# Row gathers for 32 more tokens in a product-key expert mixer: dense up products over 352 columns, 76 parked blocks, transposes in the norms

## The chip, the cores and the metric

The kernel runs on one core of a Trainium2 chip. The metric is device time in microseconds of one launch, taken as the median of several runs. The core has a matrix engine (TensorE, PE in the profile, PEld for its weight loads), a vector engine (VectorE, DVE), an activation engine (ScalarE, ACT), GpSimd (POOL) and a sync engine (SyncE, SP). Here SP issues all plain transfers, and POOL issues the gathers. The engines run their own lists of instructions in order and wait for one another by semaphores.

## What is computed

An encoder trunk of two layers over 512 tokens of width 1024. Layer 0 mixes tokens by neighbourhood attention, layer 1 by a short gated convolution. After each mixer comes the same kind of channel mixer, and nearly all of the time goes there:

```python
def peer_mixer(h, w_query, sub_keys, w_up, w_down):
    ...
        q = (xc @ w_query).reshape(c, PEER_HEADS, 2, PEER_HALF_DIM).astype(jnp.float32)
        sc = jnp.einsum('chpd,hpnd->chpn', q, keys32)
        sv, si = lax.top_k(sc, PEER_TOPK)
        cand = (sv[:, :, 0, :, None] + sv[:, :, 1, None, :]).reshape(c, PEER_HEADS, -1)
        cidx = (si[:, :, 0, :, None] * PEER_N_KEYS + si[:, :, 1, None, :]).reshape(c, PEER_HEADS, -1)
        best, pos = lax.top_k(cand, PEER_TOPK)
        eidx = jnp.take_along_axis(cidx, pos, axis=-1)
        g = jax.nn.softmax(best, axis=-1)
        u = w_up[eidx]
        a = jnp.einsum('cd,chkd->chk', xc, u).astype(jnp.float32)
        act = (jax.nn.gelu(a, approximate=False) * g).astype(xc.dtype)
        vv = w_down[eidx]
        return jnp.einsum('chk,chkd->cd', act, vv)
```

There are 8 heads with the best 16 of 256 candidates each, so every token picks 128 of 16384 experts. An expert is one row of `w_up` and one row of `w_down`, 1024 floats each. Around each mixer stands a root-mean-square norm and a residual.

## The kernel before

**Tokens.** The 512 tokens are four chunks of 128. In the expert mixer (`peer`) the last chunk (c3) gathers its rows: for each of its 128 picks one indirect transfer fetches a row of `w_up` per token, DVE multiplies it with the normed token and sums (`gather_up`, L474), and later a row of `w_down` is fetched and added with the value as weight (`gather_down`, L484). The other 384 tokens (`TD`) go densely: all 16384 experts are computed for them, in 128 blocks of 128 experts, and a gate matrix that is zero where an expert wasn't picked removes the rest.

**Exact products.** Each f32 operand is split by `split` (L100) into a high part that ACT rounds and a low part that DVE takes as the difference (L106). A product is then three products: high with high, low with high, high with low.

**Retrieval stage.** `norm_t` (L159) makes the normed, transposed activations: per chunk a reciprocal root, a diagonal `dg` with it (L168), and 32 products of the chunk with the diagonal that turn and scale at once (L174); ACT and DVE evict them as `xh` and `xl`. Then 16 query blocks follow, each with key products (`ps_k`) and the two-step top 16 on DVE (`top16`, L590). `select` (L599) then picks the experts of a chunk on DVE, in the order 3, 0, 1, 2. For the dense chunks the gates are spread over a matrix: for each four tokens (a quad) DVE makes one-hot tiles `ob` and `oa`, PE multiplies them (`ps_gb`, L457), ACT evicts to `stage`, and SP stores to `gd` in DRAM.

**Blocks ahead.** While DVE selects, PE would have little to do. So `NPRE` = 52 dense up blocks run in the meantime; their results after Gelu are stored to `ad` in DRAM (parked) and read back later as `at`. How many pieces go between two steps of the retrieval is set by estimated costs on DVE and PE and `PRE_RATE`:

```python
            for d, p in retrieval():
                dve += d
                pe += p
                while pe < dve * PRE_RATE and next(pre, 0) is None:
                    pe += 0.49
```

The framework's scheduler then settles the order on each engine.

**Main stage.** The list `blocks` mixes fresh blocks (up products still to be done, `AHEAD` = 4 early) and parked ones in groups of four. `dense_down` (L508) multiplies a block's values with the gates `gt`, splits the result and a block of `w_down`, and adds 18 products over 512 columns to six accumulators (L536). The 256 gathers of chunk 3 are spread over the blocks (L577), two shares for a fresh block and one for a parked one, through four row buffers. An up block is 24 products over 384 columns (L127) from a 512 KB load. The loads of `w_up` and `w_down` have three buffers each (`RAW`), the split results two.

## Time and profile before

| what | us |
|---|---|
| median of 3 runs | 3028.08 |
| lowest and highest run | 3024.51, 3029.07 |
| profiled execution, its own time | 3023.92 |
| span of the profiled execution | 3022.1 |
| PE, DVE, ACT, POOL busy in it | 2985.9, 2337.9, 1362.3, 658.6 |

The page slices the span into 40 equal parts. A digit is the busy share of an engine in tenths, PEclk the granted clock of TensorE, DMA the mean busy share of the 16 DMA engines. The two layers show as two repeats: first a mixer with little transfer, then retrieval with a full DVE and an idle POOL, then the long main stage with POOL's gathers and transfers near their limit. A busy PE is not PE at its peak, since its records overlap (their ends are modelled); how fast it goes is read from the distance of one start to the next.

### The profile page before, as it was taken

How to read it: one execution, taken by the hardware profiler on the slowest of the kernel's cores; microseconds unless marked ns; L12 is line 12 of the kernel's file. 1: busy time of each engine (PE TensorE's matmuls, PEld its weight loads, DVE VectorE, ACT ScalarE, POOL GpSimd, SP SyncE). 2: the span in 40 equal slices, each digit the busy share in tenths (PEclk: the TensorE clock that was granted, in tenths of full speed). 3: DMA queues.
4: the chain of work that ended last, by engine and by line, in shares of the span. 5: the costliest groups of instructions: out<-in, count | busy, mean ns of one | idle time of the engine just before them, and what ended most of it. 6: DMA issues, size and time to landing. Idle time of an engine off the chain costs nothing. (4 is left out here: it accounts for less than half of the span.)

```text
span 3022.1 us, 44124 instructions
## 1 busy us (share of the span) xinstructions
PE 2985.9 (99%) x15730; PEld 2677.1 (89%) x15730; DVE 2337.9 (77%) x5115; ACT 1362.3 (45%) x2237; POOL 658.6 (22%) x571
## 2 busy tenths in 40 slices
PE   8999999999999999999999999999999999999998
PEld 7887899999888888888888888999988888888887
DVE  4444899887888888887874489998788888888786
ACT  5444246996333333333342233599733333333333
POOL 0000000001434443443310000000034344444341
PEclk9999999999999999999999999999999999999999
DMA  4222244567999999998942323556699999999995
GB/s 162 95 97 89 87 138 159 220 233 282 340 344 340 337 344 338 333 338 316 340 144 92 108 93 114 171 196 232 239 358 340 334 348 335 340 326 350 324 332 192
DMA packets 297981, 747.96 MB, mean 247 GB/s; under 512 B 23456, under 2 KB 139168, under 8 KB 294688
## 3 DMA queue, kind: packets, MB, share of 16 engines
q1 hardware_dynamic: 224032, 476.67, 45.2%
q0 software_dynamic: 73728, 268.47, 24.0%
q8 instruction: 124, 2.03, 0.3%
q14 instruction: 97, 0.79, 0.1%
HBM read 672.17 MB, written 72.88 MB: 247 GB/s over the span
## 5 line engine op out<-in xcount | busy, mean ns | idle before, releaser
L127 PE MATMUL ps_up<-xhf,wu_l 128*128 128x384 f32 (+1 forms) x2304 | 798.9, 347 | 1.2 <-DVE wu_l L106 1.0
L127 PE MATMUL ps_up<-xhf,wu_h 128*128 128x384 f32 (+1 forms) x2304 | 794.2, 345 | 2.0 <-ACT ab L499 2.0
L127 PE MATMUL ps_up<-xlf,wu_h 128*128 128x384 f32 (+1 forms) x2304 | 792.0, 344 | 0.0
L105 ACT ACTIVATE wu_h<-wu_raw 128x1024 fp32r<-128x1024 f32 x336 | 355.4, 1058 | 710.6 <-PE ps_up L127 430.7
L470 POOL DMA_INDIRECT row<-in_up,eidx x256 | 322.4, 1260 | 1312.9 <-DMA wu_raw<-in_up_t 881.6
L536 PE MATMUL acc<-wd_h,w_l 128*128 128x512 f32 x1536 | 603.7, 393 | 0.1
L536 PE MATMUL acc<-wd_l,w_h 128*128 128x512 f32 x1536 | 599.0, 390 | 0.0
L105 ACT ACTIVATE wd_h<-wd_raw 128x1024 fp32r<-128x1024 f32 x256 | 271.6, 1061 | 702.0 <-issue 619.3
L106 DVE TENSOR_TENSOR wu_l<-wu_raw,wu_h 128x1024 fp32r<-128x1024 f32 x336 | 410.0, 1220 | 176.4 <-ACT wu_h L105 176.1
L536 PE MATMUL acc<-wd_h,w_h 128*128 128x512 f32 x1536 | 514.9, 392 | 0.0
L106 DVE TENSOR_TENSOR wd_l<-wd_raw,wd_h 128x1024 fp32r<-128x1024 f32 x256 | 313.3, 1224 | 235.5 <-ACT wd_h L105 234.9
L127 PEld LDWEIGHTS ps_up<-xhf,wu_h 128*128 128x128 f32 x2304 | 433.3, 188 | 21.1 <-ACT ab L499 3.3
L127 PEld LDWEIGHTS ps_up<-xlf,wu_h 128*128 128x128 f32 x2304 | 433.1, 188 | 17.5
L127 PEld LDWEIGHTS ps_up<-xhf,wu_l 128*128 128x128 f32 x2304 | 433.1, 188 | 17.2 <-DVE wu_l L106 3.7
L470 POOL DMA_INDIRECT row<-in_down,eidx x256 | 330.4, 1291 | 511.7 <-DVE sq L477 464.6
L536 PEld LDWEIGHTS acc<-wd_l,w_h 128*128 128x128 f32 x1536 | 288.4, 188 | 61.7
L486 DVE SCALAR_TENSOR_TENSOR accg<-row,ag,accg 128x1024 f32<-128x1024 f32 x256 | 327.4, 1279 | 16.1 <-DMA row<-in_down,eidx 15.5
L536 PEld LDWEIGHTS acc<-wd_h,w_l 128*128 128x128 f32 x1536 | 288.6, 188 | 55.0 <-DVE w_l L106 0.9
L536 PEld LDWEIGHTS acc<-wd_h,w_h 128*128 128x128 f32 x1536 | 287.2, 188 | 54.8
L477 DVE SCALAR_TENSOR_TENSOR sq<-row,hn 128x1024 bf16<-128x1024 f32 x256 | 312.0, 1219 | 3.9 <-DMA row<-in_up,eidx 2.7
L457 PE MATMUL ps_gb<-ob,oa 128*128 128x128 f32 x1536 | 209.6, 274 | 0.0
L458 ACT ACTIVATE stage<-ps_gb 128x512 f32<-128x512 f32 x192 | 204.6, 1114 | 2.1 <-PE ps_gb L457 1.5
(164 smaller groups left out, 3325.8 us busy)
## 6 DMA issues: line engine op xcount, KB each, us to landing
wd_raw<-in_down SPq DMA_DIRECT2D x256, 512.0 KB, 5.8
wu_raw<-in_up_t SPq DMA_DIRECT2D x256, 512.0 KB, 4.9
gd<-stage SPq DMA_DIRECT2D x24, 2048.0 KB, 7.4
gt<-gd SPq DMA_DIRECT2D x64, 768.0 KB, 9.2
ad<-ab SPq DMA_DIRECT2D x104, 192.0 KB, 2.1
at<-ad SPq DMA_DIRECT2D x52, 384.0 KB, 8.0
wu_raw<-in_w_query SPq DMA_DIRECT2D x32, 512.0 KB, 3.5
wu_raw<-in_w_qkv SPq DMA_DIRECT2D x24, 512.0 KB, 3.5
```

The costliest lines, as they stand in the source:

```text
L105: nc.scalar.activation(hi, raw, AF.Copy)
L106: nc.vector.tensor_tensor(lo, raw, hi.bitcast(F32), op=ALU.subtract)
L127: nc.tensor.matmul(ps[:, :n], a[:, c], b[:, kc, :n], start=k == 0, stop=k == 3 * KC - 1)
L457: nc.tensor.matmul(ps[:, n * NK:(n + 1) * NK], a, b4[:, n], start=True, stop=True)
L458: nc.scalar.activation(stage[:, :, 4 * q:4 * q + 4].rearrange("p i t -> p t i"), ps.rearrange("p (t i) -> p t i", t=4), AF.Copy)
L470: nc.gpsimd.indirect_dma_start(out=t, out_offset=None, in_=table, in_offset=bass.IndirectOffsetOnAxis(ap=eidx[:, k:k + 1], axis=0))
L477: nc.vector.scalar_tensor_tensor(o, t, 1.0, hn, op0=ALU.mult, op1=ALU.mult, accum_out=ag[:, k:k + 1])
L486: nc.vector.scalar_tensor_tensor(accg, t, ag[:, k:k + 1], accg, op0=ALU.mult, op1=ALU.add)
L536: nc.tensor.matmul(acc[c, half], aa[:, cs], ww[:, hs], start=new and i == 0, stop=n == NK - 1 and ww is held[-1][-1])
```

## The change

The last 32 tokens of the third chunk (`UT`, so the dense up products keep `TU` = 352 columns) get their values from gathered rows of `w_up`. Their down side stays dense: the value, Gelu times gate, is written into the gates `gT`, and the columns of the dense values are set to one (`ring`, `parked`). For this chunk 2 is selected first; its 32 tokens stand in a tile `hu` four times, one copy per group of 32 partitions, so that one indirect transfer brings 4 picks of 32 tokens, and 32 transfers bring all 128. `unit_steps` issues them between the steps of the other chunks' selection and multiplies on DVE; `unit_values` places the results ahead of the last group of quads. `hu` and the rows take buffers of the `w_down` splits and loads. `NPRE` goes to 76 and `PRE_RATE` to 1.52. In `norm_t` DVE scales the whole chunk (`hs`), and PE transposes it with the identity; the reciprocal root of chunk 3 is used again for `hn`.

```diff
-NPRE = 52
-PRE_RATE = 1.4
+NPRE = 76
+UN = 1
+UT = 32
+TU = TD - UN * UT
+GB = 4
+PRE_RATE = 1.52
...
-        dg = {}
-        for c in order:
-            r = rstd_of(c)
-            dg[c] = small.tile([P, P], F32, name="dg", bufs=4)
-            nc.vector.tensor_scalar(dg[c], ident, r, None, op0=ALU.mult)
-        for k0 in range(0, KC, 4):
-            ps = [ps_acc(f"ps_t{k}") for k in range(4)]
+        rs = {}
+        with tc.tile_pool(name="scaled", bufs=1) as sp:
+            hs = {}
             for c in order:
+                r = rs[c] = rstd_of(c)
+                hs[c] = sp.tile([P, D], F32, name=f"hs{c}")
+                nc.vector.tensor_scalar(hs[c], h[:, c], r, None, op0=ALU.mult)
+            for k0 in range(0, KC, 4):
+                ps = [ps_acc(f"ps_t{k}") for k in range(4)]
+                for c in order:
+                    for k in range(4):
+                        kc = k0 + k
+                        nc.tensor.transpose(ps[k][:, c * P:(c + 1) * P], hs[c][:, kc * P:(kc + 1) * P], ident)
                 for k in range(4):
                     kc = k0 + k
-                    nc.tensor.matmul(ps[k][:, c * P:(c + 1) * P], h[:, c, kc * P:(kc + 1) * P], dg[c],
-                                     start=True, stop=True)
-            for k in range(4):
-                kc = k0 + k
-                nc.scalar.activation(xh[:, kc], ps[k], AF.Copy, scale=gain[:, kc:kc + 1])
-                nc.vector.scalar_tensor_tensor(xl[:, kc], ps[k], gain[:, kc:kc + 1], xh[:, kc].bitcast(F32),
-                                               op0=ALU.mult, op1=ALU.subtract)
-        return xh, xl
+                    nc.scalar.activation(xh[:, kc], ps[k], AF.Copy, scale=gain[:, kc:kc + 1])
+                    nc.vector.scalar_tensor_tensor(xl[:, kc], ps[k], gain[:, kc:kc + 1], xh[:, kc].bitcast(F32),
+                                                   op0=ALU.mult, op1=ALU.subtract)
+        return xh, xl, rs
...
-    ad = dram.tile([NPRE // 2, P, 2, TD], F32, name="ad")
+    ad = dram.tile([NPRE // 2, P, 2, TU], F32, name="ad")
...
-            r3 = rstd_of(c3)
-            nc.vector.scalar_tensor_tensor(hn, h[:, c3], r3, hn, op0=ALU.mult, op1=ALU.mult)
+            nc.vector.scalar_tensor_tensor(hn, h[:, c3], rs[c3], hn, op0=ALU.mult, op1=ALU.mult)
+            cu = ND - 1
+            hu = []
+            for u in range(UN):
+                q = slice(P - (UN - u) * UT, P - (UN - u - 1) * UT)
+                t = wpool.tile([P, D], F32, name="hu", tag="wd_h", bufs=2)
+                nc.sync.dma_start(t[q], g_ffn_row[l].to_broadcast([UT, D]))
+                nc.vector.scalar_tensor_tensor(t[q], h[q, cu], rs[cu][q], t[q], op0=ALU.mult, op1=ALU.mult)
+                for g in range(P // UT):
+                    if g * UT != q.start:
+                        nc.scalar.activation(t[g * UT:(g + 1) * UT], t[q], AF.Copy)
+                hu.append((q, t))
...
+            fu = pp.tile([P, UN, UT], F32, name="fu")
+            xu = pp.tile([P, UN, UT], I32, name="xu")
+            gu = pp.tile([P, UN, UT], F32, name="gu")
+            au = pp.tile([P, UN, UT], F32, name="au")
+            urows = []
+            def flat_ids(eid, ii, jj):
+                nc.vector.scalar_tensor_tensor(eid, ii, float(NK), jj, op0=ALU.mult, op1=ALU.add)
+                if l:
+                    nc.vector.tensor_scalar(eid, eid, float(l * NK * NK), None, op0=ALU.add)
+            def unit_lists(gg, ii, jj):
+                flat_ids(eid, ii, jj)
+                for u, (q, _) in enumerate(hu):
+                    for g in range(P // UT):
+                        ks = slice(g * UT, (g + 1) * UT)
+                        nc.scalar.activation(fu[ks, u], eid[q, ks], AF.Copy)
+                        nc.scalar.activation(gu[ks, u], gg[q, ks], AF.Copy)
+                nc.vector.tensor_copy(xu, fu)
+            def unit_steps():
+                at = [(u, k) for u in range(UN) for k in range(UT)]
+                for n in range(len(at) + 2):
+                    if n < len(at):
+                        u, k = at[n]
+                        t = wpool.tile([P, D], F32, name="urow", tag="wd_r", bufs=RAW)
+                        nc.gpsimd.indirect_dma_start(
+                            out=t, out_offset=None, in_=up,
+                            in_offset=bass.IndirectOffsetOnAxis(ap=xu[:, u, k:k + 1], axis=0))
+                        urows.append(t)
+                    if n >= 2:
+                        u, k = at[n - 2]
+                        o = acts.tile([P, D], BF16, name="sq", tag="sq")
+                        nc.vector.scalar_tensor_tensor(o, urows.pop(0), 1.0, hu[u][1], op0=ALU.mult, op1=ALU.mult,
+                                                       accum_out=au[:, u, k:k + 1])
+                    yield
+            def unit_values():
+                nc.scalar.activation(au, au, AF.Gelu)
+                nc.vector.tensor_tensor(au, au, gu, op=ALU.mult)
+                ps = ps_acc("ps_u")
+                for u in range(UN):
+                    nc.tensor.transpose(ps[:UT, u * P:(u + 1) * P], au[:, u], ident)
+                for u in range(UN):
+                    for g in range(P // UT):
+                        ks = slice(g * UT, (g + 1) * UT)
+                        nc.scalar.activation(gT[ks, TU + u * UT:TU + (u + 1) * UT],
+                                             ps[:UT, u * P + g * UT:u * P + (g + 1) * UT], AF.Copy)
...
-                for c in (3, 0, 1, 2):
+                units = iter(())
+                for c in (cu, c3, 0, 1):
                     it = select(sv[:, c], si[:, c], pr, cand)
                     while True:
                         try:
                             yield next(it), 0.0
+                            for _ in itertools.islice(units, 1):
+                                yield 1.3, 0.0
...
-                            nc.vector.tensor_copy(t[:, c * P:(c + 1) * P], ps[:, n * P:(n + 1) * P])
+                            m = min(P, TU - c * P) if n == 0 else P
+                            nc.vector.tensor_copy(t[:, c * P:c * P + m], ps[:, n * P:n * P + m])
+                        if c == cu:
+                            unit_lists(gg, ii, jj)
+                            units = unit_steps()
                 for t0 in range(0, TD, GT):
+                    if t0 == TU:
+                        for _ in units:
+                            yield 1.3, 0.0
+                        unit_values()
...
+            ring = [pp.tile([P, TD], F32, name=f"ab{n}") for n in range(AHEAD + 2)]
+            for t in ring:
+                nc.gpsimd.memset(t[:, TU:], 1.0)
...
-                for ps in up_pieces(up_t[l, b], xh, xl, TD):
+                for ps in up_pieces(up_t[l, b], xh, xl, TU):
                     yield
-                a = pp.tile([P, TD], F32, name="ab", tag="ab", bufs=AHEAD + 2)
-                nc.scalar.activation(a, ps[:, :TD], AF.Gelu)
+                a = ring[b % len(ring)]
+                nc.scalar.activation(a[:, :TU], ps[:, :TU], AF.Gelu)
                 if b < NPRE:
-                    nc.sync.dma_start(ad[b // 2, :, b % 2], a)
+                    nc.sync.dma_start(ad[b // 2, :, b % 2], a[:, :TU])
...
-                    at = p2.tile([P, 2, TD], F32, name="at")
-                    nc.sync.dma_start(at, ad[b // 2])
+                    at = parked[b // 2 % 2]
+                    nc.sync.dma_start(at[:, :, :TU], ad[b // 2])
...
+            parked = [p2.tile([P, 2, TD], F32, name=f"at{n}", bufs=1) for n in range(2)]
+            for t in parked:
+                nc.gpsimd.memset(t[:, :, TU:], 1.0)
```

Two places where the order on an engine changes follow.

DVE, first layer, before: the second chunk's pick (`msk`) overlaps the third chunk's top 16 (`best`, `tk`, `pos`); `wu_l` is the low part of a dense up block.

```order
L637 TENSOR_TENSOR msk_4151<-msk_4151,ranks_83 128x2048
L596 MAX best_4330<-tk_4390 128x8
L596 MAX best_4330<-tk_4402 128x8
L597 MAX_INDEX pos_4331<-best_4330,tk_4368 128x8
L106 TENSOR_TENSOR wu_l_4438<-wu_raw_4435,wu_h_4437 128x1024
L638 TENSOR_TENSOR msk_4151<-msk_4151,ds_4118 128x2048
L597 MAX_INDEX pos_4331<-best_4330,tk_4390 128x8
L597 MAX_INDEX pos_4331<-best_4330,tk_4402 128x8
```

Between two splits stand only steps of the selection. The same place with the change; `urow` is a gathered row, `au` the sums.

```order
L722 TENSOR_TENSOR msk_4405<-msk_4405,ranks_83 128x2048
L464 SCALAR_TENSOR_TENSOR sq_4220,au_3619<-urow_4144,hu_2576 128x1024
L112 TENSOR_TENSOR wu_l_4528<-wu_raw_4525,wu_h_4527 128x1024
L681 MAX best_4642<-tk_4758 128x8
L681 MAX best_4642<-tk_4795 128x8
L681 MAX best_4642<-tk_4823 128x8
L723 TENSOR_TENSOR msk_4405<-msk_4405,ds_4348 128x2048
L464 SCALAR_TENSOR_TENSOR sq_4248,au_3619<-urow_4181,hu_2576 128x1024
L682 MAX_INDEX pos_4643<-best_4642,tk_4758 128x8
L682 MAX_INDEX pos_4643<-best_4642,tk_4795 128x8
L682 MAX_INDEX pos_4643<-best_4642,tk_4823 128x8
L112 TENSOR_TENSOR wu_l_4565<-wu_raw_4562,wu_h_4564 128x1024
```

Row products now stand between the selection's steps and the splits, about one per split.

SP, main stage of the first layer, before: the loads of up blocks (`wu_raw`), down blocks (`wd_raw`), gates (`gt`) and parked pairs (`at`).

```order
L516 DMA at_9880<-ad_126 128x768
L111 DMA wu_raw_10018<-in_up_t 128x1024
L111 DMA wd_raw_9635<-in_down 128x1024
L111 DMA wd_raw_9706<-in_down 128x1024
L511 DMA gt_9878<-gd_125 128x12x128
L516 DMA at_9950<-ad_126 128x768
L111 DMA wd_raw_9777<-in_down 128x1024
L111 DMA wd_raw_9846<-in_down 128x1024
L111 DMA wd_raw_9888<-in_down 128x1024
L111 DMA wu_raw_10088<-in_up_t 128x1024
```

Here one group of parked blocks stands between groups of fresh ones. And with the change, where two groups of parked blocks follow each other:

```order
L598 DMA at0_8097<-ad_126 128x2x352
L117 DMA wu_raw_10495<-in_up_t 128x1024
L117 DMA wd_raw_9943<-in_down 128x1024
L117 DMA wd_raw_9978<-in_down 128x1024
L598 DMA at1_8098<-ad_126 128x2x352
L593 DMA gt_10106<-gd_125 128x12x128
L117 DMA wd_raw_10013<-in_down 128x1024
L117 DMA wd_raw_10045<-in_down 128x1024
L598 DMA at0_8097<-ad_126 128x2x352
L117 DMA wu_raw_10569<-in_up_t 128x1024
```

There are 38 loads of parked pairs per layer instead of 26 and fewer loads of up blocks among them. On PE, 80 up blocks stand ahead of the first down product in each layer's list, 59 before.

## Rows read from the trace of the kernel before

**Rows 1.** Stretches: us, busy PE, PEld, DVE, ACT, POOL (count), clock, DMA share, GB/s.

```profile
305.00:734.00 429.00, 427.47 (x2661) 410.74 (x2660) 382.34 (x1387) 282.91 (x456) 3.90 (x4) 1.00 0.50 176
734.00:1500.00 766.00, 766.00 (x3742) 680.25 (x3741) 626.89 (x819) 274.09 (x402) 312.52 (x245) 1.00 0.94 341
1500.00:1555.00 55.00, 54.95 (x242) 44.70 (x241) 42.52 (x61) 21.73 (x32) 9.59 (x7) 1.00 0.60 210
```

**Rows 2.** Waits of PE: who, for whom, us in total, times, longest.

```profile
PE ps_t L174 <- DVE dg L168: 19.6, 4, 8.4
...
PE ps_up L127 <- DVE wu_l L106: 1.0, 4, 0.3
```

**Rows 3.** The chain that ended last: start, us, what.

```profile
2376.05 4.12 PE acc L536 x18
2380.18 4.19 PE ps_up L127 x24
```

**Rows 4.** Stretches as in the first group, in the selection of the first layer.

```profile
475.00:500.00 25.00, 24.00 (x139) 23.42 (x138) 25.00 (x98) 16.50 (x23) 0.00 (x0) 1.00 0.51 169
500.00:525.00 25.00, 25.00 (x161) 24.90 (x160) 24.22 (x62) 18.81 (x23) 0.00 (x0) 1.00 0.45 149
```

**Rows 5.** Instructions of PE in order of time: start, us, what, count.

```profile
107.22 0.66 PE L280 MATMUL ps_pt<-ident,sc 128*128 128x128 f32 x4
107.63 0.48 PE L127 MATMUL ps_up<-xlm,wu_h 128*128 128x512 f32 x1
...
600.91 1.05 PE L457 MATMUL ps_gb<-ob,oa 128*128 128x128 f32 x8
601.72 0.42 PE L127 MATMUL ps_up<-xhf,wu_l 128*128 128x384 f32 x1
...
1559.18 4.29 PE L174 MATMUL ps_t<-dg,h 128*128 128x128 f32 x36 [1.43 <-DVE dg L168]
```

**Rows 6.** Groups of DVE by line and form: busy us, mean ns, idle before.

```profile
L106 DVE TENSOR_TENSOR wu_l<-wu_raw,wu_h 128x1024 fp32r<-128x1024 f32 x336 | 410.0, 1220 | 176.4 <-ACT wu_h L105 176.1
...
L477 DVE SCALAR_TENSOR_TENSOR sq<-row,hn 128x1024 bf16<-128x1024 f32 x256 | 312.0, 1219 | 3.9 <-DMA row<-in_up,eidx 2.7
...
L477 DVE DVE_READ_ACCUMULATOR sq<-row,hn 128x1 f32 x256 | 20.9, 82 | 0.0
...
L168 DVE TENSOR_SCALAR dg<-ident,r 128x128 f32<-128x128 f32 x16 | 4.4, 282 | 0.0
L360 DVE TENSOR_SCALAR cv<-u,wc 128x512 f32<-128x512 f32 x8 | 3.9, 486 | 0.8
```

**Rows 7.** A group of ACT by line and form, as above.

```profile
L150 ACT ACTIVATE sq<-h 128x1024 bf16<-128x1024 f32 x22 | 23.1, 1052 | 13.2 <-DVE h L588 8.7 <-DMA h<-in_x 2.2 <-DVE h L583 2.0
```

**Rows 8.** Stretches as in the first group, in the norm after the attention.

```profile
284.00:290.00 6.00, 1.11 (x6) 0.58 (x4) 5.03 (x18) 5.73 (x13) 1.39 (x2) 0.86 0.79 220
290.00:295.00 5.00, 5.00 (x23) 5.00 (x24) 3.47 (x18) 1.38 (x4) 0.00 (x0) 0.50 0.22 79
295.00:300.00 5.00, 5.00 (x41) 4.78 (x40) 2.73 (x5) 3.46 (x7) 0.00 (x0) 0.98 0.02 3
```

**Rows 9.** Instructions of DVE in order of time, as for PE.

```profile
286.84 1.22 DVE L106 TENSOR_TENSOR wd_l<-wd_raw,wd_h 128x1024 fp32r<-128x1024 f32 x1
287.97 0.21 DVE L151 TENSOR_SCALAR v<-v 128x1 f32<-128x1 f32 x2
```

**Rows 10.** Issues of transfers: what, queue, count, KB each, us to landing.

```profile
at<-ad SPq DMA_DIRECT2D x52, 384.0 KB, 8.0
...
row<-in_up,eidx POOLq DMA_INDIRECT x256, 7.1
```

**Rows 11.** Stretches as in the first group, early in the two main stages.

```profile
750.00:775.00 25.00, 25.00 (x121) 21.85 (x120) 19.72 (x27) 9.01 (x13) 9.49 (x8) 1.00 1.05 408
2200.00:2225.00 25.00, 25.00 (x122) 21.94 (x121) 21.06 (x30) 8.46 (x14) 10.24 (x8) 1.00 1.01 392
```

More of the change, by code (lines that the diff above doesn't have):

```diff
@@ L204, in attention @@
     def attention(l):
-        xh, xl = norm_t(gm[:, l], f"m{l}", (3, 0, 1, 2) if l else range(NCH))
+        xh, xl, _ = norm_t(gm[:, l], f"m{l}", (3, 0, 1, 2) if l else range(NCH))
         with tc.tile_pool(name="attn", bufs=1) as ap, tc.tile_pool(name="attn2", bufs=2) as a2:
@@ L343, in short_conv @@
     def short_conv(l):
-        xh, xl = norm_t(gm[:, l], f"m{l}", (3, 0, 1, 2) if l else range(NCH))
+        xh, xl, _ = norm_t(gm[:, l], f"m{l}", (3, 0, 1, 2) if l else range(NCH))
         with tc.tile_pool(name="conv", bufs=1) as ap, tc.tile_pool(name="conv2", bufs=2) as a2:
@@ L373, in encoder @@
     gd = dram.tile([TD // GT, P, NK, GT], F32, name="gd")
-    ad = dram.tile([NPRE // 2, P, 2, TD], F32, name="ad")
+    ad = dram.tile([NPRE // 2, P, 2, TU], F32, name="ad")
     def peer(l):
-        xh, xl = norm_t(gf[:, l], f"f{l}")
+        xh, xl, rs = norm_t(gf[:, l], f"f{l}")
         with ExitStack() as st:
@@ L425, in retrieval @@
                     if c == c3:
-                        nc.vector.scalar_tensor_tensor(eid, ii, float(NK), jj, op0=ALU.mult, op1=ALU.add)
-                        if l:
-                            nc.vector.tensor_scalar(eid, eid, float(l * NK * NK), None, op0=ALU.add)
+                        flat_ids(eid, ii, jj)
                         nc.vector.tensor_copy(eidx, eid)
@@ L460, in retrieval @@
                         yield 1.35, 0.9
+                        for _ in itertools.islice(units, 1):
+                            yield 1.3, 0.0
                     nc.sync.dma_start(gd[t0 // GT], stage)
```

## The prediction, made before the changed kernel ran

> **What bounds the kernel now.** I read the busy times by stage first [rows 1]. The three stretches are the first layer's expert mixer: 305 to 734 us is the query and retrieval stage with 52 up blocks computed ahead, 734 to 1500 us the main stage, 1500 to 1555 us its end. TensorE (PE) is busy throughout, which alone says little, since its records overlap. The list of who waited for whom settles it [rows 2]: in the whole run PE waited 19.6 us for the norms' diagonals and 1.0 us for split weights, and next to nothing else. So the spacing of its instructions is the time. The chain of waits gives it [rows 3]: an up block of 24 products over 384 columns takes 4.19 us (174.6 ns each), a down block of 18 products over 512 columns 4.12 us (228.9 ns each). The program has 256 of each, so 2127 of 3022 us. What PE loses is won only where nothing else is at its limit. Two others are near: VectorE (DVE) is busy 25.00 and 24.22 of 25 us in the selection [rows 4], and the transfers move 341 GB/s at a share of 0.94 in the main stage [rows 1].
>
> **Up products over 352 columns.** Cost per column from the two forms [rows 3]: (228.9 - 174.6) / 128 = 0.424 ns. 32 columns fewer give 13.6 ns, a block 0.33 us (3.86 us after), 256 blocks 83 us. Could loading the weights hold the pace instead? Eight 128-column products, each with its own load, start within 0.81 us, 0.10 us apiece [rows 5], so no floor shows above 0.10 us and 0.161 us is free of it. In proportion to columns it would be 89 us; I take 83.
>
> **The norms.** 128 tiles were turned by a product with a diagonal, two records each: 36 records took 4.29 us [rows 5], 0.24 us a tile. A transpose is one record, and four of them are through after 0.41 us in the attention [rows 5], 0.10 us a tile. That is 17 us of PE work, but most of it lies where PE waits for the chain of squares and roots. On that chain the diagonal (0.28 us) becomes a scaled chunk of 1024 columns: from 0.28 us at 128 and 0.49 us at 512 columns [rows 6] I estimate 0.76 us, 0.5 us more, four times in a row. In the two norms ahead of the experts, ScalarE (ACT) now also makes three copies of hu, about 1.05 us each by the activation of the same 1024 columns [rows 7], ahead of the evictions that the query waits for; that eats the gain. The other two keep about 1 us each. I take -2 us, between -17 (all of it) and +10 (all four chains longer by 2 us, and some clock).
>
> About the clock: in the norm after the attention PE idles, and its granted clock reads 0.86, then 0.50 (1.2 GHz) during the turning products, then 0.98 [rows 8]. The Trainium skill (TensorE: Matmul & The Clock Gate, Part 4: PE-mode transpose) says that transposes don't count as PE activity the way products do. By that rule the first query products of each norm would run at the low level for a stretch like that one, 5 us at half speed, 2.5 us in each of four norms, and the total would be 10 us higher. The attention's transposes at 0.10 us stand among products, so no row decides it.
>
> **The selection on DVE.** Each layer gains 32 products of a gathered row with hu, as the existing gathered products 1.219 + 0.082 us [rows 6], 42 us. They sit in the stretch where DVE is already full [rows 4]. I counted the order up to the point where DVE has 16 or 17 quads of one-hots behind it: before, 30 dense splits lie ahead of it, after it 42 splits and all 32 row products. DVE gains 12 x 1.22 [rows 6] + 42 = 57 us by its records; they overlap (a split recorded at 1.22 us is followed after 1.13 us [rows 9]), so about 52. PE gains 42 x 3.86 - 30 x 4.19 = 36 us to that point. The difference, 16 us, is time in which PE waits for splits; I take 14, since DVE had a little room earlier in the stage. Later DVE has room again, but PE can't win back a wait. Bounds: 3 us (DVE room taken up in full) and 25 us (rows of the gather late, too). Two layers: +28 us.
>
> The 32 gathers themselves go by the empty GpSimd queue, beside transfers at a share of 0.50 [rows 1]. With three buffers, 1.3 us of issue, 7.1 us to land [rows 10] and 1.3 us of use, a row is ready every 3.2 us, against about 4.1 us of DVE work between two of them: hidden by 0.9 us.
>
> **76 blocks parked.** The work shifts between stages. By the order, the first down product comes after 59 up blocks before and after 80 now. Retrieval on PE alone: 429 + 21 x 4.19 - 80 x 0.33 = 491 us. Main stage: 821 - 21 x 4.19 - 48 x 0.33 = 717 us. Their sum falls by 42 us, half of the 83. The main stage now has to be fed in 717 us. It moved 766 x 0.341 + 55 x 0.210 = 272.8 MB [rows 1]. 21 up blocks fewer take away 11.0 MB; 38 reads of parked pairs at 0.360 MB for 26 at 0.393 MB [rows 10] add 3.5 MB. That leaves 265.3 MB. If the end stretch keeps its 11.6 MB in 55 us, 253.7 MB must come in 662 us: 383 GB/s, where it was 341. No long stretch shows this. One end: when prefetches pile up, 25 us went at 408 and at 392 GB/s [rows 11], so the queues can, and the main stage keeps 717 us. The other: 341 at a share of 0.94 [rows 1] means 363 at 1.00, and the stage takes 55 + 253.7/0.363 = 754 us. The share isn't linear (176 GB/s at 0.50 [rows 1] is 352 at 1.00), so I lean to the first and take 375 GB/s: 731 us, 14 us a layer, +28 in all, between 0 and 74.
>
> The Trainium skill (DMA: Bandwidth & Descriptors, Specifications) gives about 358 GB/s as one core's share of the memory; the windows at 408 and 392 lie above it, so here the measurement decides. By 358 the main stage would take 764 us and the total 66 us more than forecast, the rival on the transfers below.
>
> **Sum.** -83 - 2 + 28 + 28 and 1 us for the values of the rows (a table load, a transpose and small copies ahead of the last group, otherwise hidden): -28 us. The profiled execution took 3023.9 us (span 3022.1), so 2996; the median of the runs is 4 us above it, and I state the time beside that: 3000 us.
>
> **Rivals.** (a) PE stays the bound in the main stage: for it speak the 25-us windows and that no transfer made PE wait before. 3000 - 28 = 2972, and 2944 if DVE's lag vanishes as well. (b) The transfers can't exceed what the share says, 363 GB/s: 3000 - 28 + 74 = 3046, slower than before. For it speaks that 0.94 leaves little; against it the windows. It decides from the rate at which the main stage costs 28 us a layer: 253.7 MB in 690 us, 368 GB/s; below that the change loses. DVE can aggravate it, since late rows stop it in order, and behind a waiting sum of rows stand the splits. (c) The gathered rows for the 32 tokens come late: at 9.7 us of landing the cover is gone, at 11 us each waits 0.4 us, 14 us a layer: 3028. (d) The products don't get shorter with columns: no row speaks for it; 3083.
>
> **Chances.** The forecast (2975 to 3020) 0.38, (a) 0.30, (b) 0.17, (c) 0.08, (d) and others 0.07. A measurement tells about 0.2%, 6 us, from no change. Faster: 0.37 of the forecast, (a), and a little of (c) and (b), 0.70. Same: 0.10. Slower: most of (b), part of (c), (d): 0.20. The range, 2950 to 3045 us, reaches into (a) and to the end of (b).
>
> **What would show it.** Up blocks of 3.86 us in the chain; if 4.19, the first step falls. PE waits for split weights of about 14 us in each selection; if none, DVE's term falls. In the main stage PE waits for split weights or w, while rows and weights land later than 7.1 us, at 370 to 380 GB/s; a main stage of 717 us with 383 GB/s is (a), one of 750 us or more at about 363 is (b). The forecast is wrong, too, if row products wait for their gathers, or if the clock reads 0.50 well into the query.

## The result, and the profile after

The changed kernel took 3134.24 us (median of 4 runs, 3132.22 to 3137.39), the kernel before beside it 3028.57 us. The ratio is 1.0356 (95% interval 1.0343 to 1.0369): slower by 106 us, where 28 us faster was forecast. The profiled execution has a span of 3130.5 us, 108.4 above that of before.

The PE instructions in order of time give the marks of each layer's expert mixer: the start of the second query block, the first down product and the last one. (The products of the first query block stand among the norm's transposes, from 298 us on in both kernels; the 305 us in [rows 1] is the mark used here.) The table has the stretches between the marks, in us (the two layers with a slash); "query" is the start of that second block.

| kernel | to query | retrieval | main stage | last product to next query | last product to end |
|---|---|---|---|---|---|
| before | 305.2 | 429.0 / 429.2 | 821.3 / 820.7 | 205.0 | 12.0 |
| after | 307.0 | 510.9 / 512.5 | 712.5 / 714.3 | 288.9 | 84.4 |

Retrieval and main stage together became shorter, by 26.8 and 23.0 us. The stretches behind the products became longer, by 83.9 and 72.4 us. With 1.8 us ahead of the first query mark that is 1.8 - 49.8 + 156.3 = 108.3 us, the whole difference but for rounding. So the loss isn't in the stages that the prediction reckoned with; it stands behind the last product of each layer.

Stretches of the kernel after (us, busy PE, PEld, DVE, ACT, POOL with counts, granted clock, DMA share, GB/s), for the selection, the rest of the retrieval, the main stage and what follows it; they answer to [rows 1, 4]:

```profile
425.00:625.00 200.00, 188.11 (x1179) 184.50 (x1179) 190.19 (x553) 119.67 (x178) 41.95 (x32) 0.97 0.77 269
625.00:815.00 190.00, 190.00 (x1372) 189.99 (x1372) 148.01 (x329) 161.31 (x294) 5.10 (x6) 1.00 0.64 231
...
815.00:1530.00 715.00, 715.00 (x3473) 619.27 (x3473) 591.22 (x788) 261.51 (x383) 266.51 (x216) 1.00 0.95 342
1530.00:1620.00 90.00, 5.82 (x27) 5.01 (x26) 60.69 (x93) 7.91 (x21) 45.44 (x41) 0.53 0.67 227
```

PE is busy for all of the main stage, at the full level of its clock, with the transfers at 342 GB/s and not the 383 that were reckoned necessary. Then it has 5.82 us of work in 90, while DVE and POOL go on. The list of PE's waits says the same in one line (it answers to [rows 2]): the norm's transposes wait for the root `r`, once for 84.2 us.

```profile
PE ps_t L182 <- DVE r L159: 97.8, 3, 84.2
PE ps_up L133 <- ACT ab L581: 10.4, 11, 2.1
PE ps_up L133 <- DVE wu_l L112: 8.0, 10, 1.5
```

What runs behind the products is in the chain that ended last, here behind the second layer (start, us, what). One up block of the second main stage stands first, then pieces of the chain's last 90 us; it answers to [rows 3]:

```profile
2339.85 3.86 PE ps_up L133 x24
...
3039.79 5.51 PE acc L618 x24
3046.15 2.84 issue
3049.21 0.94 POOL row L552
...
3055.54 5.72 DMA row<-in_up,eidx
3061.29 1.25 DVE sq L559 x2
...
3067.28 5.58 DMA row<-in_down,eidx
3072.96 1.28 DVE accg L568
...
3109.18 5.15 DMA row<-in_down,eidx
3114.43 1.30 DVE accg L568
```

These are the gathers of chunk 3, the last 128 tokens, whose 256 rows per layer go through four buffers: issue, transfer, use on DVE, and a free buffer for the next. When the products end, this work isn't done. DVE's records on the tile `row` count it: 384 per layer, two for a row of w_up and one for a row of w_down (us, busy DVE with count, clock, DMA share, GB/s, in the kernel after):

```profile
818.00:1530.00 712.00, 270.05 (x328) 1.00 0.95 342
1530.00:1616.00 86.00, 50.20 (x56) 0.53 0.71 237
2331.00:3046.00 715.00, 275.02 (x332) 1.00 0.95 340
3046.00:3131.00 85.00, 45.17 (x52) 0.53 0.70 239
```

In the kernel before, all 384 lie in the first 802 of its 821 us:

```profile
734.00:1536.00 802.00, 319.52 (x384) 1.00 0.94 337
1536.00:1555.00 19.00, 0.00 (x0) 1.00 0.29 105
```

Why the gathers didn't speed up with the products is in POOL's waits:

```profile
POOL row L552 <- DVE sq L559: 462.9, 200, 6.2
...
POOL row L552 <- DVE accg L568: 412.0, 198, 6.8
```

Of the 512 gathers 398 wait for DVE to free a buffer, while DVE itself, in the first main stage, waits for a row to arrive four times, 3.9 us in all. The rows lie ready in their buffers, so by the waits it is the place of their use in DVE's instruction order that decides the pace. No run moved the uses alone, with four buffers kept. By the times of single steps more would be possible: the prediction reckons 9.7 us from a row's issue to the end of its use, so four buffers would give a row every 2.4 us (an estimate), and behind the products the rows come 2.0 us apart (last section). In the built program 212 of 256 uses stand ahead of the last block's `w` in the first layer and 215 in the second; in the kernel before it is all 256.

### The profile page after: what moved, and what is told of

It reads as the page before. It is cut to its first block, busy times and chain, and to the rows that moved or that the text cites. A ratio compares the mean times of both kernels' runs of the same rounds, so it can differ in the third digit from the quotient of the medians.

```text
span 3130.5 us, 44359 instructions
## 1 busy us (share of the span) xinstructions
PE 2907.1 (93%) x15604; PEld 2587.8 (83%) x15604; DVE 2422.8 (77%) x5242; ACT 1361.2 (43%) x2263; POOL 725.2 (23%) x651
## 5 line engine op out<-in xcount | busy, mean ns | idle before, releaser
L133 PE MATMUL ps_up<-xhf,wu_h 128*128 128x352 f32 (+1 forms) x2304 | 775.5, 337 | 14.7 <-ACT ab L581 10.4
L133 PE MATMUL ps_up<-xhf,wu_l 128*128 128x352 f32 (+1 forms) x2304 | 771.3, 335 | 8.1 <-DVE wu_l L112 8.0
L133 PE MATMUL ps_up<-xlf,wu_h 128*128 128x352 f32 (+1 forms) x2304 | 771.7, 335 | 0.0
L618 PE MATMUL acc<-wd_h,w_l 128*128 128x512 f32 x1536 | 595.1, 391 | 0.0
L618 PE MATMUL acc<-wd_l,w_h 128*128 128x512 f32 x1536 | 578.2, 392 | 0.0
L618 PE MATMUL acc<-wd_h,w_h 128*128 128x512 f32 x1536 | 489.6, 392 | 1.6 <-ACT wd_h L111 1.6
L552 POOL DMA_INDIRECT row<-in_down,eidx x256 | 307.5, 1201 | 487.6 <-DVE sq L559 448.9
```

The costliest lines, as they stand in the source:

```text
L133: nc.tensor.matmul(ps[:, :n], a[:, c], b[:, kc, :n], start=k == 0, stop=k == 3 * KC - 1)
L552: nc.gpsimd.indirect_dma_start(out=t, out_offset=None, in_=table, in_offset=bass.IndirectOffsetOnAxis(ap=eidx[:, k:k + 1], axis=0))
L618: nc.tensor.matmul(acc[c, half], aa[:, cs], ww[:, hs], start=new and i == 0, stop=n == NK - 1 and ww is held[-1][-1])
```

## The experiments

**Theory A**: chunk 3's gathers, with four buffers, keep about the pace that they had, 821/256 = 3.2 us per row. The main stage became some 108 us shorter (parked blocks and shorter products), and what it no longer covers runs alone. **Rival B**: the transfers set the end, and the tail is only the form in which their lack shows. All ratios are to the kernel before on the same chip; its medians there were 3025 to 3027 us.

**Six buffers.**

```diff
-RING = 4
+RING = 6
```

> The changed kernel with six row buffers for chunk 3's gathers instead of four; nothing else. Theory A (the gather chain of chunk 3 sets the end: four buffers keep it at about 3.2 us per row, so that the products of the main stage, 713 us long now, end with 41 to 53 rows still to go, which then run alone, 84 us per layer): the two tails go and nothing takes their place, so 3134 - 2 x about 80 = about 2975 us (2955 to 3000), last product within 10 us of the end. Rival B (the transfers set the end: 383 GB/s are needed when gathers keep pace with products, and the stage before the change moved at most 363 GB/s averaged over its length): the tail goes, but the products are held up by late weights, main stage 717 x 383/363 = about 757 us instead of 713, so about 3050 us, with PE waits on the weight tiles in the main stage. If neither holds (the buffers are not what holds the gathers): 3134.

Measured: 3053.52 us, ratio 1.0087 (1.0066 to 1.0109). Retrieval 512.3 / 515.4, main stage 749.4 / 744.4, then 206.4 and 11.8: both tails are gone, as A says, and the time fell by 81 us. But the main stages grew by 37 and 30 us, as B says, and the time is near B's 3050 (its stage of 757 us is somewhat long); A's 2975 was missed. Stretch of the main stage, as above, and PE's waits of the whole run:

```profile
815.00:1530.00 715.00, 690.33 (x3348) 596.47 (x3348) 607.93 (x808) 252.97 (x371) 329.06 (x247) 1.00 0.98 358
```

```profile
PE acc L618 <- ACT wd_h L111: 43.4, 27, 3.4
```

Once the gathers keep pace the transfers are nearly full (0.98), at 358 GB/s over 715 us, and PE waits for late weights. In the changed kernel that wait comes to 1.6 us in the whole run, and in the first main stage PE waits for nothing.

**Five buffers**, a dose between.

> The changed kernel with five row buffers. The instruction order of the program leaves 33 and 36 rows behind the last block, instead of 44 and 41. Theory A: a dose between four and six: 16 rows fewer in the tails at 1.64 us each, so 3134 - 26 = about 3108 us (3085 to 3120). Rival B: what the gathers do earlier the weights lose, so 3134 or above. Where the buffers don't matter: 3134.

Measured: 3097.32 us, 1.0235 (1.0218 to 1.0252). The stretches behind the products are 257.6 and 66.3 us, so the tails fell from 156 to 107 us, and the main stages are 722.6 and 717.8. This is A's order; the saving per row was more than reckoned.

**Six buffers in the kernel before**, nothing else. Expected before it ran: by Theory A nothing is won, 3020 to 3030 us, since its gathers already end with its products; if more buffers by themselves make a better or worse order, 10 us or more to either side of 3025.

```diff
-RING = 4
+RING = 6
```

Measured: 3024.69 us, ratio 0.9993 (0.9983 to 1.0003), no difference. DVE's records on `row` lie in the same 802 us:

```profile
734.00:1536.00 802.00, 319.55 (x384) 1.00 0.93 338
```

So the buffers didn't hold the gathers in the kernel before. The program spreads the 256 rows over 0.97 of its blocks (`LATE`), which asks for one every 3.1 us of the 821, and with four and with six buffers the uses on DVE come 3.1 us apart and end 21 to 22 us ahead of the last product. In the changed kernel the same rule asks for 2.7 us; with four buffers the uses in its main stages come 3.2 to 3.3 us apart, with five 3.2, with six 2.9. The 3.2 us of Theory A is thus about what the orders with four buffers reach when they are asked for more, and the old stage was just long enough for it.

**76 blocks parked in the kernel before**, nothing else of the change.

```diff
-NPRE = 52
-PRE_RATE = 1.4
+NPRE = 76
+PRE_RATE = 1.52
```

> The kernel before with 76 blocks parked instead of 52 and the new rate of parking; all else old (384 columns, no gathered rows of w_up, old norms). The order of the program leaves 28 and 25 rows behind the last block. Theory A: parking moves 24 x 4.19 = 100 us of products per layer out of the main stage into the retrieval, the gathers stay at their pace, so 37 and 34 rows (9 more than in the order) run behind the products at 1.64 us each, 58 us per layer: 3028 + 116 = about 3140 us (3090 to 3150), with no other change. Rival B: the stage is short of transfers and its products wait: about 3100, with waits of PE on weights and no tail. If the loss comes from the gathered rows of w_up or the norms, this kernel is at 3028.

Measured: 3137.1 us, 1.0368 (1.0351 to 1.0385). DVE's records on `row`, as above, from the first layer:

```profile
830.00:1564.00 734.00, 286.04 (x346) 1.00 0.95 341
1564.00:1620.00 56.00, 30.27 (x32) 0.53 0.66 215
```

The same slowdown comes from the parking alone: tails of 54.6 and 42.5 us, and 14 us more in the retrievals and main stages (523.2 + 734.3 and 521.0 + 735.3). The old columns, norms and row counts stand in this kernel, so none of the other three edits is needed for the loss.

**The change with 52 blocks parked.**

```diff
-NPRE = 76
+NPRE = 52
-PRE_RATE = 1.52
+PRE_RATE = 1.4
```

> The changed kernel with 52 blocks parked instead of 76 and the old rate of parking: the 352 columns, the gathered rows of w_up and the transposes stay. The order of the program leaves 5 and 1 rows behind the last block; on the chip some 9 more were left in the changed kernel than in its order. Theory A: the main stage is 76 x 0.33 = 25 us shorter than before the change, 796 us, and the gathers need 256 x 3.2 = 820 us less what runs quicker in the tail, so tails of 10 to 20 us per layer remain: 3028 - 83 (columns) + 28 (selection on DVE) + 30 (tails) = about 3003 us (2980 to 3030). Rival B (transfers): at 52 blocks the stage asks for about 350 GB/s, which it had before, so no loss: 2973. A third view, that the gathered rows of w_up or the new norms are what costs: still 3100 or more.

Measured: 3059.78 us, 1.0117 (1.01 to 1.0134): above A's range. The tails are small, as A said (215.0 and 12.6 us behind the products, 11 us over before), and the main stages 792.6 and 791.2. The miss is in the retrieval: 464.9 / 471.9 us against 429, where shorter products should have made it shorter. That opened a second question, to which the last two runs answer.

**Half of each gathered row**, six buffers (the row numbers are doubled for it, and the buffers' other half is set to zero).

```diff
-                    out=t, out_offset=None, in_=table,
+                    out=t[:, :D // 2], out_offset=None, in_=table.rearrange("n (a d) -> (n a) d", a=2),
```

> The changed kernel with six row buffers in which each gather of chunk 3 fetches only the first 512 of a row's 1024 values (2 KB instead of 4 KB; the row buffers' other half is zero). The same number of gathers, the same work on every engine; what it leaves out is half of the gathered bytes, so the outputs of chunk 3 are not the reference's. It asks what the six-buffer version (3053) still loses in its main stages, 749 and 744 us against 713 with four buffers. Theory T (once the gathers keep pace, the transfers set the stage: it moved 362 to 370 GB/s for long stretches and its products waited for late weights): with 67 MB fewer per stage the stage is back at 713 to 720 us and no tail comes, so 3053 - 65 = about 2988 us (2975 to 3000). Rival S (six buffers let the scheduler put gather work ahead of the splits of the weights on DVE, so it's the order on DVE that delays the products): the bytes don't matter, about 3050 us.

Measured: 2989.6 us, 0.9878 (0.9861 to 0.9894). Main stages 717.0 and 718.1 us, no tail:

```profile
818.00:1530.00 712.00, 708.41 (x3436) 612.11 (x3435) 636.63 (x851) 262.24 (x387) 351.87 (x252) 1.00 0.83 276
```

With the number of gathers and of their uses kept and only bytes left out, the 30 us that six buffers had added to each main stage vanish but for 4. The transfers set that stage, not the order on DVE; theory T holds.

**60 blocks parked**, six buffers, rate 1.45.

> The changed kernel with six row buffers and 60 blocks parked (rate 1.45) instead of 76. The order of the program leaves no row behind the last block. The version with 52 parked left PE without work near the end of the retrieval (8.7 us of busy time in the 25 us from 750 to 775) and the one with 76 ran its main stage at the transfers' limit; between them both should have about what they can do. Theory T: retrieval 465 to 475 us as with 52 parked (83 us shorter idle filled by 8 blocks), main stage 792 - 8 x 3.86 = 761 us, which asks for about 361 GB/s, so a few us of late weights: 1241 per layer against 1250 before, so 3025 - 18 + 5 = about 3012 us (2995 to 3030). If the retrieval's length is set by DVE's work alone and each parked block adds its own splits to it, 490 us of retrieval and 3040.

Measured: 3060.68 us, 1.012 (1.01 to 1.0139): a miss. Retrieval 486.3 / 490.4, main 780.2 / 774.0. PE had run out of parked blocks again towards the end of the retrieval, and then waited for the table and the weights of the first down block:

```profile
750.00:800.00 50.00, 30.03 (x191) 27.09 (x191) 30.04 (x72) 29.82 (x60) 8.65 (x10) 0.83 0.62 238
```

```profile
PE acc L618 <- DMA gt<-gd: 14.5, 1, 14.5
PE ps_up L133 <- DVE wu_l L112: 15.1, 9, 4.8
PE acc L618 <- ACT w_h L111: 13.8, 1, 13.8
```

**The old norms with six buffers.** The diagonal products come back, the rest stays.

> The changed kernel with six row buffers and the norms as they were before the change (products with the diagonal tile in place of one-pass transposes of scaled copies); all else as in the six-buffer version (3053). The order leaves 1 row behind the last block. Theory N (what the sum assumed): the norms are worth -2 us, between -17 and +10 over the four of them, so 3045 to 3065. Rival: the scaled copies on DVE and the transposes at the low granted clock cost more than the diagonal products, by 3 us per norm or over: 3040 or below.

Measured: 3035.06 us, 1.0029 (1.0019 to 1.0038), 18 us below its twin with the new norms. Only 4.1 us of that lie ahead of the first query mark; 8.6 lie in the retrievals and 5.9 in the main stages, where no norm runs. So this pair doesn't price the norms, and the next kernel was made for that.

**The new norms in the kernel before**, alone.

```diff
-            dg[c] = small.tile([P, P], F32, name="dg", bufs=4)
-            nc.vector.tensor_scalar(dg[c], ident, r, None, op0=ALU.mult)
+                hs[c] = sp.tile([P, D], F32, name=f"hs{c}")
+                nc.vector.tensor_scalar(hs[c], h[:, c], r, None, op0=ALU.mult)
...
-                    nc.tensor.matmul(ps[k][:, c * P:(c + 1) * P], h[:, c, kc * P:(kc + 1) * P], dg[c],
-                                     start=True, stop=True)
+                        nc.tensor.transpose(ps[k][:, c * P:(c + 1) * P], hs[c][:, kc * P:(kc + 1) * P], ident)
```

> The kernel before with the one-pass transposes of scaled copies in its four norms; nothing else of the change. The version with six buffers was 18 us slower with them (3053) than with the diagonal products (3035), but only 4 us of that lie in the stretch that ends with the second norm; the rest lies in retrievals and main stages. Theory N (the prediction's term): -2 us, so 3024 (3009 to 3036). Rival M (the new norms cost what the pair of six-buffer versions shows): 3026 + 18 = 3044 us. Between them, 3028 to 3034: the norms cost the 4 us seen, and the rest of the 18 is how the order of instructions falls.

Measured: 3019.45 us, ratio 0.9977 (0.9967 to 0.9986): 7 us faster. The query mark comes at 303.0 us instead of 305.2, the stretch between the layers takes 202.1 instead of 205.0, retrieval and main stage are as before (429.1 and 821.0). So in the profiled runs two norms together save 2 to 3 us, 5 us in all of the 7 between the medians, and Rival M is out for the norms by themselves. This part of the change alone is a kernel that beats both.

**32 rows of chunk 3 gathered in the retrieval**, six buffers, old norms: bytes moved from the stage that is full into the one with room. The places that call `early_steps` are left out here.

```diff
+            def early_steps():
+                got = []
+                for n in range(EARLY + 2):
+                    if n < EARLY:
+                        t = wpool.tile([P, D], F32, name="erow", tag="wd_r", bufs=RAW)
+                        fetch(up, n, t)
+                        got.append(t)
+                    if n >= 2:
+                        up_value(n - 2, got.pop(0))
+                    yield
```

> The changed kernel with six row buffers, the old norms (3035), and 32 of chunk 3's 128 rows of w_up gathered in the retrieval, behind the gathered rows of chunk 2, instead of in the main stage. 32 x 0.52 MB = 16.8 MB per layer leave a stage that moves about 363 GB/s and go into one that moves 230 to 245 GB/s. Theory T (transfers set the main stage): it loses 16.8 MB / 363 GB/s = 46 us of transfers, which is more than the 30 us that it stands above the products alone, so 745 becomes 713 to 722; DVE's 32 x 1.3 = 42 us move into a retrieval in which it is idle for about 45 us from 600 to 815 us, for 0 to 10 us per layer: 3035 - 2 x 25 + 2 x 5 = about 2995 us (2975 to 3010), faster than both kernels. If transfers aren't what holds the stage, or DVE has no room in the retrieval: 3035 to 3070.

Measured: 3056.25 us, 1.0102 (1.0086 to 1.0119). The main stages did what T says, 717.5 and 713.8 us instead of 745.6 and 742.3. The retrievals lost more than that: 544.8 / 553.4 instead of 507.3 / 511.8. The room on DVE that I had seen there was no room for PE: the one-hot products wait for DVE and ACT, PE runs out of parked blocks, and then 14 us pass until the first down product has its `w`.

```profile
800.00:850.00 50.00, 32.93 (x241) 31.77 (x240) 31.19 (x75) 35.10 (x67) 4.54 (x7) 0.89 0.59 213
```

```profile
PE acc L637 <- ACT w_h L112: 28.4, 2, 14.6
PE acc L637 <- ACT wd_h L112: 23.8, 15, 1.9
PE ps_gb L536 <- ACT oa L532: 12.9, 18, 1.4
```

**The same with the new norms.**

> The same 32 early gathers with the new norms and six row buffers (3053 without the early gathers). Theory T: as for the kernel with the old norms, 3053 - 50 = about 3000 us (2985 to 3020). Beside its twin with the old norms: theory N has the two within 10 us of each other, rival M has this one 18 us later.

Measured: 3053.77 us, 1.0091 (1.0074 to 1.0107), retrieval 545.0 / 552.3, main 715.0 / 714.1. The same result as its twin, 2 us apart, so here too the norms don't cost 18 us. Where the 18 us between the two six-buffer kernels without early rows come from stays open; their orders differ in more places than the norms.

**52 blocks parked, six buffers**, and the same **without the gathered rows of w_up** (their sums are set to 0.5):

```diff
-                        nc.gpsimd.indirect_dma_start(
-                            out=t, out_offset=None, in_=up,
-                            in_offset=bass.IndirectOffsetOnAxis(ap=xu[:, u, k:k + 1], axis=0))
...
-                        nc.vector.scalar_tensor_tensor(o, urows.pop(0), 1.0, hu[u][1], op0=ALU.mult, op1=ALU.mult,
-                                                       accum_out=au[:, u, k:k + 1])
```

> The changed kernel with 52 blocks parked (rate 1.4, as before the change) and six row buffers: what is left of the change is the 352 columns, the gathered rows of w_up and the norms. With four buffers it took 3060 us, of which about 11 us were rows that ran behind the last products of the first layer, and 10 to 12 at the end. Theory A: those tails go, 3040 to 3052. If 3060 again, the tails were not theirs.

> As the one above, without the 32 gathers of w_up rows per layer and without their 32 products on DVE (their values are set to a constant, so the outputs of 32 tokens are not the reference's); the lists, the copies and the planner's allowance for them stay. It asks what the gathered rows cost and whether the shorter products are worth the forecast 83 us. Theory D (in the selection DVE sets the retrieval's length, and each product of a gathered row is 1.3 us more of DVE: 32 x 1.3 = 42 us per layer): the retrieval goes from 465 and 472 us to about 425 to 430, and the time to 3046 - 2 x 42 = about 2962 us (2940 to 2980). Rival P (the retrieval is longer because the parked products don't fill PE once they are shorter, or because of the wait for the written-back tables at its end): the gathered rows cost under 15 us, 3030 or more.

Measured: 3061.28 us, 1.0122 (1.0105 to 1.0139), and without the rows 3021.34 us, 0.9984 (0.9975 to 0.9994). The small tails went as expected (206.4 and 11.9 us behind the products), but the time didn't fall, since the rest became 11 us longer, most of it the second main stage (798.6 after 791.2) and the first retrieval (469.1 after 464.9). The gathered rows cost 40 us in the two layers. Theory D's 84 us is too much, Rival P's 15 too little: the retrieval fell from 469.1 / 473.5 to 451.3 / 452.8 us, not to 429. Stretches of the selection and of the end of the retrieval, with the rows and without:

```profile
500.00:600.00 100.00, 92.65 (x588) 90.23 (x587) 96.35 (x234) 59.83 (x89) 21.70 (x20) 0.98 0.84 284
...
700.00:750.00 50.00, 42.32 (x290) 36.97 (x288) 49.10 (x130) 48.78 (x103) 0.00 (x0) 1.00 0.47 190
```

```profile
500.00:600.00 100.00, 98.99 (x661) 98.32 (x660) 72.25 (x160) 67.21 (x108) 0.00 (x0) 1.00 0.58 195
...
700.00:750.00 50.00, 35.74 (x238) 30.20 (x236) 40.59 (x112) 43.81 (x93) 0.00 (x0) 0.98 0.49 201
```

In the selection PE gets its work back (99 of 100 us instead of 93). Further on it has too little: the shorter parked blocks are used up, and each quad of one-hot products waits 0.2 us for ACT's `oa`. PE's timeline of the kernel without the rows shows the last of them (start, us, what; idle before and what ended it in brackets), and then 13.8 us without work at the stage's border:

```profile
740.79 1.23 PE L523 MATMUL ps_gb<-ob,oa 128*128 128x128 f32 x8 [0.18 <-ACT oa L519]
742.19 1.23 PE L523 MATMUL ps_gb<-ob,oa 128*128 128x128 f32 x8 [0.17 <-ACT oa L519]
757.23 2.90 PE L607 MATMUL acc<-wd_h,w_h 128*128 128x512 f32 x6 [13.81 <-ACT w_h L111]
```

That wait for the first down product's `w` comes once per layer, 28.2 us for both layers in this run and 28.0 in the first one with 52 parked. So what the shorter columns save in the retrieval wasn't collected there, while the main stages have their part: 792.6 and 793.9 us against 821. Whether another rate of parking collects it wasn't tried.

## Why the prediction was wrong, step by step

**Up products over 352 columns: right.** A block takes 3.86 us, as forecast, and the main stages took 712.5 and 714.3 us where products alone were put at 717. The 83 us are there on PE. In the main stages they are collected (76 blocks at 0.33 us are 25 us, 27 to 30 were seen with 52 parked, and 22 in one main stage). In the retrieval they are collected only as long as PE has parked blocks left beside the one-hot products; with 76 it has, with 52 and 60 it had not.

**The norms: right within the bounds, by themselves.** Forecast -2 us between -17 and +10, measured -7 in the kernel before. In the changed kernel, with its copies of `hu`, the query mark comes 1.8 us later than before, and of the two six-buffer kernels the one with the new norms has it 4.1 us later; so there they gained nothing ahead of that mark. Granted clock in that edit alone, from 290 us on in steps of 5:

```profile
290.00:295.00 5.00, 3.83 (x18) 3.86 (x19) 4.17 (x22) 2.00 (x7) 0.00 (x0) 0.50 0.22 88
295.00:300.00 5.00, 4.95 (x27) 4.00 (x26) 3.79 (x6) 4.51 (x8) 0.44 (x1) 0.88 0.00 0
300.00:305.00 5.00, 5.00 (x23) 4.10 (x22) 2.86 (x4) 0.23 (x1) 0.52 (x1) 1.00 0.29 105
```

Against [rows 8] it is 0.88 for 0.98 in the second step, and full speed in the third. In the kernel after, with hu's copies behind the norm, the same three steps read 0.67, 0.67 and 0.65, and PE works for only 2.87 of 5 us in the second. The rule of the Trainium skill that I had weighed (TensorE: Matmul & The Clock Gate, Part 4: PE-mode transpose) agrees in direction with the kernel after, whose query starts at the low level of 1.2 GHz in part; its 10 us didn't come in the edit alone, which gained 7. No run here separates the transposes from the idle time beside them.

**The selection on DVE: near in size, not in what PE waited for.** Forecast were 14 us of waiting for split weights per layer. PE's busy time from 425 to 625 us is 188.11 of 200, so 12 us are missing there. But only 2.5 of them are waits for splits; 5.5 are waits for ACT's evictions (`ab`), the rest lies in other short waits. That the sum comes near 14 is in part luck. The retrievals took 510.9 and 512.5 us, 20 and 21 over PE's 491. The gathered rows as a whole cost 40 us in two layers in the version with 52 parked, where +28 and +1 were reckoned. Their gathers were mostly in time, as the prediction said: in the kernel after, DVE waited for such a row 8 times of 64, 12.2 us in both layers.

**76 blocks parked: the step that failed, twice.** The prediction says "The main stage now has to be fed in 717 us" and then counts bytes. It never counted turns; the gathers' own chain was put at nothing, without a reason. 256 rows had gone through four buffers in 800 of the 821 us, 3.1 us each, with 21 us to spare: a chain beside a bound PE that the program spread over the stage, shown neither by PE's waits nor by the chain that ended last, since it ended ahead of the products. In a stage that asked for 2.7 us the order with four buffers reached 3.2 to 3.3, and 40 and 36 rows were left when the last product started. The missing term is 156 us (83.9 + 72.4). The built program had it: of 256 uses in a layer 44 and 41 stand behind the last block's `w`, none before. The prediction read the order only as far as the selection.

Beside it, the rate of the transfers was mis-sized. I took 375 GB/s from two windows of 25 us [rows 11]. Where the gathers do keep pace, with six buffers, the stage ran at 358 GB/s for 715 us at a share of 0.98, and each stage took 744 to 749 us instead of the forecast 731. In the prediction's own terms (253.7 MB ahead of an end stretch of 55 us) that is 365 to 368 GB/s, near (b)'s 363. The short windows hold for 25 us and not for 700. The Trainium skill's figure (DMA: Bandwidth & Descriptors, Specifications, about 358 GB/s for one core), which I had set aside for them, agrees with the 358 of the long stretch; but that is a mean, pieces of 100 us of it read 339 to 370 GB/s, and no run here shows that the figure is a limit.

**The rivals.** (a), PE as the bound in the main stage, is what the trace after shows of that stage: without the 156 us behind the products its span would be 2974, where (a) said 2972. That nearness is luck: (a) has the stage fed at 383 GB/s with all its rows, and it moved 342 without 40 of them; where the rows keep pace, PE waits for weights. (b), transfers at 363 GB/s, with 3046, is what the six-buffer version does (3053, main stages 744 to 749 for its 754). Both described stages; neither had the tail, and no case of mine had the end at 3134. Of (c) there is a small part, the 12.2 us that DVE waited for gathered rows, for its 28; (d) fails by the 3.86 us. The chance of 0.20 for slower was built on (b), with parts of (c) and (d).

**No version with the columns that does all the work beat the kernel before.** PE's products sum to 491 + 717 = 1208 us per layer, 42 below before, but then three others are at their end: DVE in the selection, the transfers in the main stage, and the one-hots' chain over DVE and ACT when parked blocks are lacking. Retrieval and main stage sum to 1250 us in the kernel before; to 1260 to 1262 with six buffers, 1253 to 1254 with the old norms, 1257 to 1272 with 52 or 60 parked, 1260 to 1267 with early rows. With all gathers inside these stages, only leaving out bytes (1228 to 1235) or rows (1244 to 1247) brought the sum below. What is faster than both kernels is the norm edit alone, by 7 us.

## What to carry to other kernels

When a stage is to become shorter, list every chain that runs beside its bound, divide its length by its steps, and compare that with what the shorter stage will ask for. A chain that just fits is a candidate for the next bound, though no wait of the bound engine names it. Whether it can go faster has to be tried in the shortened stage: here two more buffers changed nothing in the old kernel and took 81 us off the changed one. For a chain through a few buffers, count in the built program how many of its steps stand behind the last step of the stage. A rate that must hold for a whole stage is taken from the longest stretch at a high share, not from the fastest short window.

## What was not expected of the hardware

Alone, with the same four buffers, the rows follow each other at under two thirds of the spacing that they have in the main stage: in the tail of the first layer DVE takes eight of them from 1560.07 to 1574.05 us, 2.0 us apart with all waits (DVE's instructions in order of time, the first and the last of the eight):

```profile
1560.07 1.28 DVE L568 SCALAR_TENSOR_TENSOR accg<-row,ag,accg 128x1024 f32<-128x1024 f32 x1 [0.67 <-DMA row<-in_down,eidx]
...
1574.05 1.23 DVE L559 SCALAR_TENSOR_TENSOR sq<-row,hn 128x1024 bf16<-128x1024 f32 x1 [0.29 <-DMA row<-in_up,eidx]
```

There DVE does wait for the rows, 23 times and 24.4 us in the 86, where in the main stage it did so four times. A single transfer in the chain of the tail takes 5.0 to 6.1 us; it was 7.1 at the median beside the weights [rows 10]. In the 86 us of the first tail the granted clock reads 0.53; it is back at 1.00 at 1622 us, 7 us after the first transpose.
